# A two-block transformer on one core: the last weight tile of each chunk in other parts or in another order

## Chip, cores and metric

The kernel runs on 1 core of one Trainium2 chip. The metric is the device time of one execution in microseconds (us); lower is better.

## What is computed

The reference runs two blocks of two layers each over 256 tokens of width 1024, in float32. The first block is a gated MLP mixer, a gated feed-forward layer with a short convolution, banded attention and another feed-forward layer; the second is a mixer of attention and a recurrence, a feed-forward layer with an embedding gate, latent attention and another feed-forward layer. Nearly all of the arithmetic is products of activations with weight matrices:

```python
h = h + gmlp_mixer(rmsnorm(h, a_norm_g[l]), a_w_in[l], a_v_norm_g[l], a_w_s[l], a_b_s[l], a_w_out[l])
...
h = h + chunk_attention(rmsnorm(h, b_norm_g[j]), k_shared, v_shared, b_w_q[j], b_rel_bias[j], b_w_o[j])
h = h + conv_ffn(rmsnorm(h, f_norm_g[l]), f_w_in[l], f_conv_w[l], f_conv_b[l], f_w_down[l])
...
mix = sb_rwkv_mixer(hn, hyb_w_in[j], ...)
mix = mla_mixer(hn, positions, mla_w_down[j], ...)
h = h + conv_glu(rmsnorm_2(h, ffn_norm[i]), ffn_w_in[i], ffn_conv_w[i], ffn_conv_b[i], ffn_w_out[i])
```

## The kernel before, in words

Activations stand with their 1024 features on the partitions, in 8 tiles of 128, and the 256 tokens as columns. All weight matrices are cut into tiles of 128x128 and packed on the host, in the order of use, into 399 **chunks** of 8 tiles (128 partitions x 1024 columns, 512 KB). `w()` hands out the next tile and has the chunk two ahead (`LOOK`) prepared by `_chunk` (L406): SP issues the DMA into `raw`, ACT rounds it into `whi` (type fp32r, L418), DVE makes the remainder `wlo = raw - whi` (L419). `raw` has four buffers, `whi` and `wlo` three each. Activations are split in the same way into `xh` and `xl` (L496, L497; `hh` and `hl` in the second half of a feed-forward layer). `self.spec` is the list of the tiles handed out so far.

A product of a weight tile with an activation tile is then three products on TensorE that add up in PSUM: high weight by high activation, high weight by low activation, low weight by high activation. `gemm_tile` (L439) issues them with the weights stationary and the 256 tokens as moving columns; `self.mm` (L384) is the one line, L385, through which nearly all products of the program pass. `gemm_rows` does the same with the activations stationary and 512 weight columns moving, four tiles at a time. In the profile a product is named output <- moving, stationary operand (`g<-xh,wlo`), and each product has its own load of the stationary operand, LDWEIGHTS, listed under PEld.

PE runs in program order throughout (`pe_order`, L460); the mixers have hand-written lists of steps (`GMLP_ORDER` and others), which interleave chunks' products with the small products of the mixers. In the two layers of `ffn1`, ACT and DVE too run in program order; everywhere else a scheduler places their instructions. `gated_layer` (L800) runs the feed-forward layers: 22 pairs of output tiles with 8 weight tiles each, then the down projection over 22 tiles of `hh` and `hl`.

Of the kernel before, what the change touches and what calls it, by code (L numbers as in the profile page):

```python
# [21 lines left out]
S = 256  # L22
# [4 lines left out]
CT = 8  # L27
# [296 lines left out]
class Net:  # L324
# [114 lines left out]
    def gemm_tile(self, X, ps, name, idx, cols, first=True, k0=0, ks=None, n=None):  # L439
        n = n or len(X)  # L440
        for k in range(*(ks or (0, n))):
            xh, xl = X[k]
            wh, wl = self.w(name, idx, k0 + k * P, cols)
            self.mm(ps, wh, xh, start=first and k == 0, stop=False)
            self.mm(ps, wh, xl, start=False, stop=False)
            self.mm(ps, wl, xh, start=False, stop=k == n - 1)

    def gemm_pair(self, X, ps, name, idx, parts, late=False, mid=None, at=0):

# [1276 lines left out]
```

## Time and profile before

| | us |
|---|---|
| median of 3 runs (1316.29 to 1318.71) | 1318.56 |
| the profiled execution, its own time | 1321.39 |
| span of its instructions | 1319.6 |
| PE busy (10864 products) | 1292.5 |
| PEld busy (10864 loads of weights) | 1231.4 |
| DVE busy | 1026.5 |
| ACT busy | 781.9 |

The times in the table are of one core. PE's busy time is the union of its products' recorded durations, which overlap: a product of 256 columns is recorded with some 280 ns, while the next one starts 113 to 118 ns later. How fast PE goes is read from the starts, or from the length of a run of products divided by their number.

### The profile page before, as it was taken

How to read it: one execution, taken by the hardware profiler on the slowest of the kernel's cores; microseconds unless marked ns; L12 is line 12 of the kernel's file. 1: busy time of each engine (PE TensorE's matmuls, PEld its weight loads, DVE VectorE, ACT ScalarE, POOL GpSimd, SP SyncE). 2: the span in 40 equal slices, each digit the busy share in tenths (PEclk: the TensorE clock that was granted, in tenths of full speed). 3: DMA queues.
4: the chain of work that ended last, by engine and by line, in shares of the span. 5: the costliest groups of instructions: out<-in, count | busy, mean ns of one | idle time of the engine just before them, and what ended most of it. 6: DMA issues, size and time to landing. Idle time of an engine off the chain costs nothing.

```text
span 1319.6 us, 27125 instructions
## 1 busy us (share of the span) xinstructions
PE 1292.5 (98%) x10864; PEld 1231.4 (93%) x10864; DVE 1026.5 (78%) x2037; ACT 781.9 (59%) x1359; POOL 16.1 (1%) x48
## 2 busy tenths in 40 slices
PE   7999999999999999999999999999999999999997
PEld 5999999988899999999876799999998989999997
DVE  5889997566679998578964488897779978889656
ACT  6667665457667665448343266665557766665544
POOL 0000000000000000001100000000000000000000
PEclk9999999999999999999998799999999999999998
DMA  7566555555446556574440056565555436665551
GB/s 271 176 225 193 189 189 182 189 187 177 132 145 192 191 180 190 191 237 145 124 129 18 17 167 206 192 190 182 189 176 161 127 113 189 193 198 181 191 182 60
DMA packets 70398, 223.18 MB, mean 169 GB/s; under 512 B 13408, under 2 KB 15712, under 8 KB 70272
## 3 DMA queue, kind: packets, MB, share of 16 engines
q1 hardware_dynamic: 63312, 212.43, 50.3%
q10 hardware_dynamic: 6192, 5.34, 1.4%
q0 software_dynamic: 768, 3.67, 0.8%
q8 instruction: 85, 1.39, 0.4%
q14 instruction: 41, 0.34, 0.1%
HBM read 218.53 MB, written 2.88 MB: 168 GB/s over the span
## 4 chain that ended last, share of the span: by engine, by line
PE 92%; DVE 4%; DMA 2%; ACT 1%; issue 1%; SPq 0%; ACTq 0%; DVEq 0%
PE g L385 78%; PE s L385 6%; PE t L385 3%; PE o L385 3%; PE t L783 1%; DVE wlo L419 1%; DMA raw<-in_wall 0%; DMA b<-dZ 0%; DVE tm L1217 0%; ACT whi L418 0%; DMA dA<-b 0%; DVE sqa L171 0%; DVE xl L497 0%; DVE tm L1219 0%; DMA tm<-dA 0%
## 5 line engine op out<-in xcount | busy, mean ns | idle before, releaser
L385 PE MATMUL g<-xh,whi 128*128 128x256 f32 x2184 | 618.0, 283 | 1.4 <-ACT xh L496 1.4
L385 PE MATMUL g<-xl,whi 128*128 128x256 f32 x2184 | 610.3, 279 | 2.5 <-DVE xl L497 2.4
L419 DVE TENSOR_TENSOR wlo<-raw,whi 128x1024 fp32r<-128x1024 f32 (+1 forms) x400 | 487.8, 1221 | 160.4 <-ACT whi L418 157.4
L418 ACT ACTIVATE whi<-raw 128x1024 fp32r<-128x1024 f32 (+1 forms) x400 | 421.9, 1055 | 317.4 <-PE g L385 172.5
L385 PE MATMUL g<-xh,wlo 128*128 128x256 f32 x2184 | 609.6, 279 | 0.1
L385 PEld LDWEIGHTS g<-xh,whi 128*128 128x128 f32 x2184 | 410.7, 188 | 7.2 <-issue 4.0
L385 PEld LDWEIGHTS g<-xl,whi 128*128 128x128 f32 x2184 | 410.9, 188 | 4.0 <-DVE xl L497 3.3
L385 PEld LDWEIGHTS g<-xh,wlo 128*128 128x128 f32 x2184 | 414.1, 190 | 0.3 <-DVE wlo L419 0.3
L385 PE MATMUL g<-hh,wlo 128*128 128x256 f32 x704 | 197.8, 281 | 0.0
L385 PE MATMUL g<-hl,whi 128*128 128x256 f32 x704 | 197.8, 281 | 0.0
L385 PE MATMUL g<-hh,whi 128*128 128x256 f32 x704 | 197.8, 281 | 0.0
L385 PEld LDWEIGHTS g<-hh,wlo 128*128 128x128 f32 x704 | 135.2, 192 | 0.0
L385 PEld LDWEIGHTS g<-hh,whi 128*128 128x128 f32 x704 | 132.2, 188 | 0.0
L385 PEld LDWEIGHTS g<-hl,whi 128*128 128x128 f32 x704 | 132.2, 188 | 0.0
L277 ACT ACTIVATE hh<-pr 128x256 fp32r<-128x256 f32 x88 | 36.0, 409 | 48.7 <-DVE pr L272 48.7
L496 ACT ACTIVATE xh<-h,vec 128x256 fp32r<-128x256 f32 x80 | 39.1, 499 | 24.0 <-DVE h L560 20.9
L867 ACT ACTIVATE c<-pad,vec 128x256 f32<-128x256 f32 x88 | 47.7, 590 | 9.4 <-DVE pad L856 9.4
L874 DVE SCALAR_TENSOR_TENSOR c<-pad,vec,c 128x256 f32<-128x256 f32 x88 | 42.7, 485 | 3.1
L497 DVE SCALAR_TENSOR_TENSOR xl<-h,vec,xh 128x256 fp32r<-128x256 f32 x80 | 37.9, 481 | 6.9 <-ACT xh L496 6.8
L872 DVE SCALAR_TENSOR_TENSOR c<-pad,vec,c 128x256 f32<-128x256 f32 x88 | 42.2, 480 | 0.0
L282 DVE TENSOR_TENSOR hl<-pr,hh 128x256 fp32r<-128x256 f32 x88 | 36.9, 420 | 3.9 <-ACT hh L277 3.9
L385 PE MATMUL g<-whi,xh 128*128 128x512 f32 x68 | 29.1, 428 | 9.2 <-ACT xh L496 9.2
(375 smaller groups left out, 1396.1 us busy)
## 6 DMA issues: line engine op xcount, KB each, us to landing
raw<-in_wall SPq DMA_DIRECT2D x398, 512.0 KB, 3.5
bias<-in_bias POOLq DMA_DIRECT2D x4, 768.0 KB, 7.1
cst_c<-in_c ACTq DMA_DIRECT2D x1, 896.0 KB, 7.1
raw<-in_wall SPq DMA_DIRECT2D x2, 256.0 KB, 4.1
h<-in_x ACTq DMA_DIRECT2D x2, 256.0 KB, 4.3
h<-in_x POOLq DMA_DIRECT2D x2, 256.0 KB, 7.6
ws<-in_ws ACTq DMA_DIRECT2D x1, 512.0 KB, 8.7
bs<-in_bs ACTq DMA_DIRECT2D x1, 512.0 KB, 8.8
```

What stands on the lines that cost most here:

```text
L277: self.net.nc.scalar.activation(self.H[-1][0], self.pr, AF.Copy)
L282: self.net.nc.vector.tensor_tensor(hl, self.pr, hh.bitcast(F32), ALU.subtract)
L385: self.nc.tensor.matmul(out, lhsT=lhsT, rhs=rhs, start=start, stop=stop, skip_group_check=True)
L418: nc.scalar.activation(hi[:, s], raw[:, s], AF.Copy)
L419: self.after(nc.vector.tensor_tensor(lo[:, s], raw[:, s], hi[:, s].bitcast(F32), ALU.subtract))
L496: self.nc.scalar.activation(xh, h, AF.Copy, scale=gain)
L497: self.nc.vector.scalar_tensor_tensor(xl, h, gain, xh.bitcast(F32), ALU.mult, ALU.subtract)
L783: self.nc.tensor.transpose(pt[:, b * P:b * P + P], w[:, s * P:s * P + P], self.cst["ident"])
L867: a.activation(c0, pad[:, j, 2:], AF.Identity, bias=self.col("f_conv_b", (l,), j * KF + i), scale=cw(2, j))
L872: v.scalar_tensor_tensor(c1, pad[:, j, 1:S + 1], cw(1, j), cc[n], ALU.mult, ALU.add)
L874: v.scalar_tensor_tensor(cc[n], pad[:, j, 0:S], cw(0, j), c1, ALU.mult, ALU.add)
```

## The change

In `gemm_tile` the tile that is the last of its chunk (`o == CT - 1`) is treated by the chunk's number modulo 8 (`form`). With 0 nothing changes. With 1, 2, 3, 6 and 7 the third product, `wlo` by `xh`, is issued in two parts over the token columns: 128+128, 192+64, 64+192, 240+16 and 16+240. With 4 the order of the three is low-high, high-high, high-low, with 5 high-high, low-high, high-low. All other tiles, and `gemm_rows`, are as before.

```diff
--- before.py
+++ after.py
@@ -441,9 +441,20 @@
         for k in range(*(ks or (0, n))):
             xh, xl = X[k]
             wh, wl = self.w(name, idx, k0 + k * P, cols)
-            self.mm(ps, wh, xh, start=first and k == 0, stop=False)
+            at, o = divmod(len(self.spec) - 1, CT)
+            new, end = first and k == 0, k == n - 1
+            form = at % 8 if o == CT - 1 else 0
+            if form in (4, 5):
+                self.mm(ps, *((wl, xh) if form == 4 else (wh, xh)), start=new, stop=False)
+                self.mm(ps, *((wh, xh) if form == 4 else (wl, xh)), start=False, stop=False)
+                self.mm(ps, wh, xl, start=False, stop=end)
+                continue
+            self.mm(ps, wh, xh, start=new, stop=False)
             self.mm(ps, wh, xl, start=False, stop=False)
-            self.mm(ps, wl, xh, start=False, stop=k == n - 1)
+            cut = {1: 128, 2: 192, 3: 64, 6: 240, 7: 16}.get(form, S)
+            for c in (slice(0, cut), slice(cut, S)):
+                if c.start < S:
+                    self.mm(ps[:, c], wl, xh[:, c], start=False, stop=end)
 
     def gemm_pair(self, X, ps, name, idx, parts, late=False, mid=None, at=0):
```

By the built program 233 third products are cut (48 in 128+128, 93 in 192+64 or 64+192, 92 in 240+16 or 16+240) and the order changes in 93 chunks. Lines behind L452 stand 11 lines further down in the changed kernel.

On PE, in the first mixer, at the end of a chunk whose number is 7 modulo 8 (`g` is the sum in PSUM, `xh` and `xl` the activation's parts, `whi` and `wlo` the chunk's), the order before is this:

```order
L385 MATMUL g_738<-xl_257,whi_626 128x256
L385 MATMUL g_738<-xh_256,wlo_627 128x256
L385 MATMUL g_738<-xh_264,whi_626 128x256
L385 MATMUL g_738<-xl_265,whi_626 128x256
L385 MATMUL g_738<-xh_264,wlo_627 128x256
L385 MATMUL g_785<-xh_574,whi_683 128x256
```

and with the change:

```order
L385 MATMUL g_742<-xl_257,whi_629 128x256
L385 MATMUL g_742<-xh_256,wlo_630 128x256
L385 MATMUL g_742<-xh_264,whi_629 128x256
L385 MATMUL g_742<-xl_265,whi_629 128x256
L385 MATMUL g_742<-xh_264,wlo_630 128x16
L385 MATMUL g_742<-xh_264,wlo_630 128x240
L385 MATMUL g_790<-xh_577,whi_686 128x256
```

The chunk's last product of 256 columns has become one of 16 and one of 240 with the same weights; nothing else on PE has moved.

On PE a little earlier, at the end of a chunk whose number is 4 modulo 8, the order before is this (`t<-ws,vt` is a small product of the mixer that follows the chunk):

```order
L385 MATMUL g_584<-xl_257,whi_499 128x256
L385 MATMUL g_584<-xh_256,wlo_500 128x256
L385 MATMUL g_584<-xh_264,whi_499 128x256
L385 MATMUL g_584<-xl_265,whi_499 128x256
L385 MATMUL g_584<-xh_264,wlo_500 128x256
L385 MATMUL t_615<-ws_138,vt_143 128x128
```

and with the change:

```order
L385 MATMUL g_587<-xl_257,whi_500 128x256
L385 MATMUL g_587<-xh_256,wlo_501 128x256
L385 MATMUL g_587<-xh_264,wlo_501 128x256
L385 MATMUL g_587<-xh_264,whi_500 128x256
L385 MATMUL g_587<-xl_265,whi_500 128x256
L385 MATMUL t_618<-ws_138,vt_143 128x128
```

The product with `wlo` now stands two products earlier; their number is the same.

On ACT in the same mixer, where the scheduler places the work (`whi<-raw` prepares a chunk, `xh<-gs` the high part of a gated activation, `u<-u` the activation function), the order before is this:

```order
L418 ACTIVATE whi_586<-raw_585 128x1024
L642 ACTIVATE u_570<-u_568 128x512
L509 ACTIVATE xh_574<-gs_572 128x256
L509 ACTIVATE xh_580<-gs_578 128x256
L418 ACTIVATE whi_626<-raw_625 128x1024
L418 ACTIVATE whi_683<-raw_682 128x1024
L509 ACTIVATE xh_661<-gs_659 128x256
L642 ACTIVATE u_657<-u_655 128x512
L509 ACTIVATE xh_667<-gs_665 128x256
```

and with the change:

```order
L418 ACTIVATE whi_589<-raw_588 128x1024
L520 ACTIVATE xh_577<-gs_575 128x256
L653 ACTIVATE u_573<-u_571 128x512
L520 ACTIVATE xh_583<-gs_581 128x256
L418 ACTIVATE whi_629<-raw_628 128x1024
L520 ACTIVATE xh_664<-gs_662 128x256
L418 ACTIVATE whi_686<-raw_685 128x1024
L653 ACTIVATE u_660<-u_658 128x512
L520 ACTIVATE xh_670<-gs_668 128x256
```

The first `xh` has moved ahead of an activation function and the third ahead of the preparation of a chunk; the instructions are the same. ACT's order differs in some 35 places of this kind in the whole program and DVE's in some 60; SP's order of transfers is the same, and POOL's has one instruction moved by two places.

## Rows read from the trace of the kernel before

**Rows 1.** The page's busy times: us, share of the span, number of instructions.

```profile
PE 1292.5 (98%) x10864; PEld 1231.4 (93%) x10864; DVE 1026.5 (78%) x2037; ACT 781.9 (59%) x1359; POOL 16.1 (1%) x48
```

**Rows 2.** The page's chain that ended last, by engine and by line.

```profile
PE 92%; DVE 4%; DMA 2%; ACT 1%; issue 1%; SPq 0%; ACTq 0%; DVEq 0%
PE g L385 78%; PE s L385 6%; PE t L385 3%; PE o L385 3%; PE t L783 1%; DVE wlo L419 1%; DMA raw<-in_wall 0%; DMA b<-dZ 0%; DVE tm L1217 0%; ACT whi L418 0%; DMA dA<-b 0%; DVE sqa L171 0%; DVE xl L497 0%; DVE tm L1219 0%; DMA tm<-dA 0%
```

**Rows 3.** PE's waits: for whom, us in total, times, longest us.

```profile
PE g L385 <- ACT xh L496: 10.7, 2, 9.2
PE t L385 <- DMA b<-dZ: 2.5, 2, 2.0
PE g L385 <- DVE xl L497: 2.4, 2, 1.6
...
PE t L783 <- DVE tm L1314: 0.2, 1, 0.2
```

**Rows 4.** The same view, ACT and DVE waiting before a chunk's conversions.

```profile
ACT whi L418 <- PE g L385: 172.5, 149, 2.9
DVE wlo L419 <- ACT whi L418: 157.4, 200, 5.0
```

**Rows 5.** The chain in order of time: start us, length us, products in it.

```profile
92.14 178.41 PE g L385 x1509
...
271.23 0.69 PE t L385 x3
...
790.06 0.43 PE t L385 x2
790.49 18.05 PE g L385 x159
...
862.94 10.88 PE g L385 x96
873.82 0.34 PE s L385 x4
874.16 11.42 PE g L385 x96
885.58 0.43 PE t L385 x2
...
886.01 90.45 PE g L385 x768
...
1156.89 16.32 PE g L385 x144
...
1197.64 90.45 PE g L385 x768
```

**Rows 6.** Stretches: length, PE busy (products), granted clock, DMA share, GB/s.

```profile
95.00:270.00 175.00, 175.00 (x1484) 1.00 0.58 187
680.00:720.00 40.00, 39.23 (x499) 0.92 0.10 33
720.00:770.00 50.00, 49.13 (x328) 0.76 0.11 35
```

**Rows 7.** Groups of weight loads: busy us, mean ns | idle before, by whom.

```profile
L385 PEld LDWEIGHTS g<-xh,wlo 128*128 128x128 f32 x2184 | 414.1, 190 | 0.3 <-DVE wlo L419 0.3
L385 PEld LDWEIGHTS g<-xl,whi 128*128 128x128 f32 x2184 | 410.9, 188 | 4.0 <-DVE xl L497 3.3
L385 PEld LDWEIGHTS g<-xh,whi 128*128 128x128 f32 x2184 | 410.7, 188 | 7.2 <-issue 4.0 <-ACT xh L496 1.6 <-ACT whi L418 0.3
```

**Rows 8.** Timeline of weight loads (PEld): start us, recorded us, instruction.

```profile
48.72 0.97 PEld L385 LDWEIGHTS t<-ws,vt 128*128 128x128 f32 x8
49.61 0.19 PEld L385 LDWEIGHTS g<-xh,whi 128*128 128x128 f32 x1
...
276.21 0.19 PEld L385 LDWEIGHTS g<-whi,xh 128*128 128x128 f32 x1
276.32 0.19 PEld L385 LDWEIGHTS g<-whi,xl 128*128 128x128 f32 x1
```

## The prediction

> **What bounds the kernel now.** I read the busy times first, then the chain of work that ended last, then PE's waits, and last the timeline of PE and of its weight loads. TensorE is busy for 1292.5 us of a span of 1319.6 us [rows 1], and 92% of the chain is PE, 78% in the product groups `g` of L385 [rows 2]. PE's idle time has few causes: 10.7 us for ACT `xh`, of which one wait of 9.2 us is the start of the program, 2.5 us for a DMA, 2.4 us for DVE `xl`, and smaller ones [rows 3]. The queues that feed it are early: ACT idles 172.5 us before `whi` until PE gives a buffer back, and DVE idles 157.4 us before `wlo` [rows 4]. So what is added to PE's stream is added to the time, almost without discount, and what moves on ACT and DVE costs only where it makes PE wait.
>
> The spacing of PE's products is what matters, not their recorded duration. The pieces of the chain [rows 5] give it: 1509 products in 178.41 us are 118.2 ns each, 768 in 90.45 us are 117.8 ns, but 144 in 16.32 us are 113.3 ns, all of the same form, 256 columns against 128x128 weights, three per weight tile. **There are two cadences**, about 117.8 and 113.3 ns, and a stretch keeps the one it has until other products come between. Eight long pieces of the slow one, from the one at 92.14 to the one at 1197.64, hold 5129 products, eleven of the fast one, with the last at 1156.89, hold 1629. Over both that is (5129 x 117.8 + 1629 x 113.3) / 6758 = 116.7 ns a product. It is no matter of the granted clock, which is 1.00 in a slow stretch too [rows 6].
>
> Every product is preceded by its own load of weights; two products in a row with the same `whi` load it twice (LDWEIGHTS `g<-xh,whi` and `g<-xl,whi`, x2184 each) [rows 7]. The load for the next product runs under the present one. **How long a load takes** is seen where the products are too short to hide it: eight 128x128 loads of `ws` start at 48.72 and the next load at 49.61, 0.111 us each; the load at 276.21, behind products of one column and of the type in question, is followed by the next at 276.32, 0.11 again [rows 8]. I take 0.112 and, within the rounding of these rows, 0.109 as the lower end: nearly the whole 113 to 118 ns of a product of 256 columns. The present stream has no room for a second load under one product.
>
> **The change, part by part.** (1) *The split.* 233 third products are cut in two: 48 into 128+128, 93 into 192+64 or 64+192, 92 into 16+240 or 240+16 columns. No column is added; 233 loads and 233 products are. A part of 16 to 240 columns needs less PE time than the load that must come before the next product: the product of 512 columns takes 0.23 us (three in 0.69 us [rows 5]), so 0.45 ns a column, and even 240 columns are 0.108 us. So both parts last as long as a load, 0.112 us each, and wherever the cut lies the pair takes 0.224 us in place of 0.1167: 0.107 us more. 233 x 0.107 = **25.0 us**. The lower bound goes by the shortest load and the slow cadence, 2 x 0.109 - 0.1178 = 0.100 us, 23.3 us; the upper by the fast cadence, 2 x 0.112 - 0.1133 = 0.111 us, 25.8 us. Below these lies only the case in which the second load is hidden (a rival). I count all of it on the path: in the long pieces of rows 5, which hold most of the chunks, PE runs without a gap, and from 680 to 720 us, where hardly a weight is moved (33 GB/s [rows 6]), no cut lies by the order of the program.
>
> The Trainium skill ("TensorE: Matmul & The Clock Gate", LDWEIGHTS) puts a weight load at its columns over 1.2 GHz, 107 ns for 128; the measured 0.11 us agrees. The same page (Back-to-back issue gap) gives a product of N columns N/2.4 + 2.5 ns when it stands by itself, by which a cut would cost only the second 2.5 ns, an estimate of 0.6 us in all; that is the first rival in its words.
>
> (2) *The order.* In 93 chunks the three products of the last tile change places; same products, same loads. `wlo` is wanted up to two products (0.23 us) earlier; PE's loads wait 0.3 us in all for `wlo` today [rows 7], and `whi` and `wlo` come back to their pools at most 0.23 us later in a chunk of 24 products, 2.8 us. Cover for this is the idle time in front of both conversions [rows 4]. I take 0; if the cover were gone, 93 x 0.23 would be 21 us, but nothing in rows 4 points there.
>
> (3) *The moved work on ACT and DVE.* Where the queues are placed by the scheduler and not in program order (the mixers and the layers of ffn2), ACT and DVE get another order in some 35 and 60 places, mostly by one or two instructions, as in the fence on ACT; SP keeps its order. Each place can take away or add a wait of PE. The trace shows such waits of 0.2 to 1.6 us; the ten rows of this view without the start are 11 us in all (first and last in [rows 3]), so no more than a few us can be won. I take one such wait more, **+1.5 us**, bounds -3 and +6.
>
> (4) *The cadence.* A cut breaks the rhythm of loads, and the rhythm after a break is one of the two. If the shares stay as they are this term is 0, and I take 0. It is the largest unknown: the two bounds are the rivals below.
>
> (5) *The clock.* From 680 to 770 us the granted clock averages 0.92 and then 0.76 [rows 6], half speed in parts, about 15 us lost. Shifts of where these fall may change it by a few us either way: 0, bounds -3 and +3.
>
> Sum: 25.0 + 0 + 1.5 + 0 + 0 = 26.5 us. The profiled execution took 1321.39 us (span 1319.6 and 1.8 around it), 2.8 above the median of the three runs, 1318.56; added to the median: **1345 us**.
>
> **Rivals.** *Only columns count* (chance 0.05): the second load, of weights that are already there, is hidden or skipped. For it: the second part needs no new weights. Against it: today's pair on the same `whi` pays in full, 113 to 118 ns per product. It gives 1318.6 + 1.5 = 1320 us.
>
> *The slow cadence spreads* (0.31): after products that are shorter than a load, the trace goes on slowly: behind the four one-column products at 873.82 the 96 at 874.16 take 11.42 us, 119 ns each, where the 96 before them took 10.88 [rows 5]. If all cuts act so, the 1629 fast products of the long pieces lose 4.5 ns each, 7.3 us: 1352 us, up to 1357 with term 3 at its bound.
>
> *The fast cadence spreads* (0.10), the rival on the other side: a cut every few chunks throws the stream out of the slow rhythm. For it: behind the two products at 790.06 that are not of this kind the stream turns from slow to fast, and stays so for 159 products in 18.05 us [rows 5]; against it: the same two products at 885.58 leave it slow. 5129 x 4.5 ns = 23.1 us would come back. With the split at its lower bound and no new wait that is 1318.6 + 23.3 - 23.1 = 1319 us, not slower; it decides for "not slower" only if nearly every slow product turns fast. With half of them turned it is 1334 us.
>
> *The short parts run as plain fp32* (0.04): a product of plain fp32 with 128 columns takes two records of 0.11 us [rows 8]. If a part of fewer than 256 columns were done so, each part would be 0.22 us or more, the pair 0.33 us longer, 233 x 0.33 = 77 us: 1396 us. No product of this type with fewer than 256 columns stands in the trace, so it can't be excluded by a row.
>
> **How the numbers follow.** Forecast (shares of the cadences about as now, partly mixed) 0.50, slow spreads 0.31, fast spreads 0.10, only columns 0.05, plain fp32 0.04. The forecast's own range is 1336 to 1353. With half of the slow products turned fast at the lower end, and the slow rival with its bounds at the upper, the range for 8 in 10 is 1330 to 1358; outside are the rest of the fast rival, the columns rival and plain fp32. A measurement of this kernel tells about 0.2% (2.6 us) from no change. Slower: forecast, slow rival, plain fp32 and a part of the fast rival, 0.88. Within 0.2%: most of the columns rival and of the full fast rival, 0.08. Faster: 0.04.
>
> **What would show it.** PE has 233 products and loads more, 11097. Around a cut the loads stand 0.11 us apart and the two parts together take 0.22 us, at 128+128 as at 16+240: that shows term 1 right; 0.12 would show the columns rival. In chunks of changed order the spacing stays 113 to 118 ns. Spacings of long pieces show the cadence: the 16.32 us of 144 products growing to over 17 for the slow rival, the 178.41 us of 1509 shrinking (less their cuts) for the fast one. PE's waits in all should stay near 20 us. A total waiting of PE over 27 us would show term 3 undersized. The prediction is wrong if the pair's length depends on the cut, or if one cadence takes over.

## The result, and the profile after

The changed kernel takes 1323.27 us (median of 6 runs, 1322.58 to 1326.09) against 1318.63 us of the kernel before beside it: 1.0055 times as long, 95% interval 1.003 to 1.008. It is slower, as forecast, but by 4.6 us and not by 26.5, and 1323 lies below the range that was given. The profiled execution took 1323.33 us, with a span of 1321.5 us.

The page's busy times of the kernel after answer to [rows 1]: 233 products and 233 loads more, and PE only 1.5 us busier.

```profile
PE 1294.0 (98%) x11097; PEld 1234.9 (93%) x11097; DVE 1026.8 (78%) x2037; ACT 786.4 (60%) x1359; POOL 15.3 (1%) x48
```

PE's waits in the kernel after (for whom, us in total, times, longest us) answer to [rows 3]. All rows of this view sum to 20.9 us, before to 20.7. Single waits have changed places: the one for a DMA (2.5 us) is gone, and one for DVE `f` (2.0 us) and one for `wlo` (1.5 us) are new.

```profile
PE g L385 <- ACT xh L507: 10.8, 2, 9.2
PE s L385 <- DVE f L1193: 2.0, 1, 2.0
PE s L385 <- DVE dg L556: 1.6, 1, 1.6
PE g L385 <- DVE wlo L419: 1.5, 1, 1.5
...
PE g L385 <- DVE xl L508: 0.6, 1, 0.6
```

The chain of the kernel after in order of time (start us, length us, products) answers to [rows 5].

```profile
93.31 176.52 PE g L385 x1548
...
807.17 16.81 PE g L385 x148
...
885.17 89.52 PE g L385 x788
...
1199.35 89.52 PE g L385 x788
```

These rows hold the whole story when they are laid beside those of before. Four cuts in a piece that was fast already: 144 products in 16.32 us have become 148 in 16.81, which is 0.49 us or **0.1225 us a cut**. Twenty cuts in a piece that was slow: 768 products in 90.45 us have become 788 in 89.52. The piece is *shorter* by 0.93 us although twenty cuts were put into it. At 113.37 ns, the fast cadence, 768 products take 87.07 us (as they do in two traces below), and 87.07 + 20 x 0.1225 = 89.52. So the 748 whole and 20 cut products all run at the fast cadence now. The same for the longest piece: 1509 products would take 171.1 us fast, 39 cuts add 4.8, together 175.9; the row shows 176.52, and the 0.6 us between are in the row of before too (178.41 against 1509 x 117.8 = 177.8).

The timeline of the weight loads of the kernel after, around a cut into 192 and 64 columns and around one into 240 and 16 (start us, recorded us):

```profile
901.37 0.19 PEld L385 LDWEIGHTS g<-xl,whi 128*128 128x128 f32 x1
901.49 0.30 PEld L385 LDWEIGHTS g<-xh,wlo 128*128 128x128 f32 x2
901.71 0.19 PEld L385 LDWEIGHTS g<-xh,whi 128*128 128x128 f32 x1
901.82 0.19 PEld L385 LDWEIGHTS g<-xl,whi 128*128 128x128 f32 x1
901.94 0.19 PEld L385 LDWEIGHTS g<-xh,wlo 128*128 128x128 f32 x1
902.06 0.19 PEld L385 LDWEIGHTS g<-xh,whi 128*128 128x128 f32 x1
...
904.33 0.30 PEld L385 LDWEIGHTS g<-xh,wlo 128*128 128x128 f32 x2
904.55 0.19 PEld L385 LDWEIGHTS g<-xh,whi 128*128 128x128 f32 x1
904.66 0.19 PEld L385 LDWEIGHTS g<-xl,whi 128*128 128x128 f32 x1
904.79 0.19 PEld L385 LDWEIGHTS g<-xh,wlo 128*128 128x128 f32 x1
```

The two loads of a cut (`x2`) take 0.22 us together at either place, and the next two or three starts are 0.11 to 0.13 us apart before the stream is at 0.113 again.

Counted over the whole trace, of the steps from the start of one product of 256 columns to the start of the next, 6004 were slow (about 116 to 123 ns, 117.8 in the mean) and 2777 fast (113 to 115 ns, 113.4 in the mean) before. After, 1413 are slow and 6767 fast, and 439 of those slow ones stand within four products of a cut and so belong to its price. That leaves 974 slow steps in place of 6004: 5030 x 4.43 ns = **22.3 us come back**, against 233 x 0.1225 = **28.5 us** for the cuts.

The rest is in the stretch with the half clock. In the kernel after the granted clock is 1.00 and 0.83 where it was 0.92 and 0.76 [rows 6]:

```profile
95.00:270.00 175.00, 175.00 (x1535) 174.70 (x1535) 148.56 (x237) 108.09 (x168) 0.00 (x0) 1.00 0.62 188
680.00:720.00 40.00, 39.23 (x523) 28.22 (x522) 21.36 (x52) 18.54 (x38) 0.00 (x0) 1.00 0.13 40
720.00:770.00 50.00, 49.23 (x343) 39.24 (x344) 29.48 (x85) 17.44 (x41) 0.23 (x3) 0.83 0.17 53
```

If the products that are in both traces are matched one by one, the second trace gains 5.4 us on the first between the products at 697 and at 755 us, where half speed (1.2 GHz) was granted for 30.7 us before and for 17.1 us after. 28.5 - 22.3 - 5.4 = +0.8 us for the two profiled executions, whose spans differ by 1.9; the 1.1 us left over is not taken apart here. Whether the clock's part belongs to the change is asked below.

### The profile page after: what moved, and what is told of

Its sections match the earlier page's. It is cut to its first block, busy times and chain, and to the rows that moved or that the text cites. A ratio compares the mean times of both kernels' runs of the same rounds, so it can differ in the third digit from the quotient of the medians.

```text
span 1321.5 us, 27588 instructions
## 1 busy us (share of the span) xinstructions
PE 1294.0 (98%) x11097; PEld 1234.9 (93%) x11097; DVE 1026.8 (78%) x2037; ACT 786.4 (60%) x1359; POOL 15.3 (1%) x48
## 4 chain that ended last, share of the span: by engine, by line
PE 91%; DVE 5%; ACT 2%; issue 1%; DMA 1%; ACTq 0%; SPq 0%; DVEq 0%
PE g L385 78%; PE s L385 5%; PE t L385 4%; PE o L385 3%; DVE wlo L419 2%; PE t L794 1%; ACT whi L418 1%; DMA raw<-in_wall 0%; ACT e L736 0%; DVE xl L508 0%; DVE sqa L171 0%; DVE tm L1134 0%; DMA dA<-b 0%; DVE ple_g L993 0%; DVE f L1083 0%
## 5 line engine op out<-in xcount | busy, mean ns | idle before, releaser
L385 PE MATMUL g<-xh,wlo 128*128 128x256 f32 (+4 forms) x2354 | 607.5, 273 | 1.5 <-DVE wlo L419 1.5
L385 PE MATMUL g<-xl,whi 128*128 128x256 f32 x2184 | 603.2, 277 | 0.7 <-DVE xl L508 0.6
L385 PEld LDWEIGHTS g<-xh,wlo 128*128 128x128 f32 x2354 | 427.2, 188 | 1.7 <-DVE wlo L419 1.7
L385 PE MATMUL g<-hh,wlo 128*128 128x256 f32 (+4 forms) x760 | 195.4, 272 | 0.0
L385 PE MATMUL g<-hl,whi 128*128 128x256 f32 x704 | 193.5, 276 | 0.0
L507 ACT ACTIVATE xh<-h,vec 128x256 fp32r<-128x256 f32 x80 | 39.1, 500 | 34.5 <-DVE h L571 30.7
L878 ACT ACTIVATE c<-pad,vec 128x256 f32<-128x256 f32 x88 | 47.8, 590 | 12.5 <-DVE pad L867 12.4
L953 ACT ACTIVATE c<-pad,vec 128x256 f32<-128x256 f32 x44 | 26.5, 601 | 20.9 <-DVE pad L943 18.5
```

The source lines that it names most:

```text
L385: self.nc.tensor.matmul(out, lhsT=lhsT, rhs=rhs, start=start, stop=stop, skip_group_check=True)
L507: self.nc.scalar.activation(xh, h, AF.Copy, scale=gain)
L878: a.activation(c0, pad[:, j, 2:], AF.Identity, bias=self.col("f_conv_b", (l,), j * KF + i), scale=cw(2, j))
L953: a.activation(c0, pad[:, 1, 2:], AF.Identity, bias=self.col("ffn_conv_b_2", (l,), i), scale=cw(2))
```

## Experiments

The theory after the traces, **theory A**: a cut costs about 0.11 us (0.1225 by the rows above) and leaves PE's stream in the fast cadence, which lasts up to the next products of another kind. Rivals: **B**, a cut costs almost nothing and what follows is untouched, or it is the new order that sets the cadence; **C**, any added product does it; **D**, it takes the pair of parts; **E**, the order and the moved work on ACT and DVE cost waits of their own.

| kernel | cuts | slow steps | median us | ratio to before, 95% interval |
|---|---|---|---|---|
| before (profiled) | 0 | 6004 | 1318.63 | |
| the change | 233 | 1413 | 1323.27 | 1.0055 (1.003 to 1.008) |
| order alone | 0 | 5811 | 1317.59 | 1.0036 (1.0008 to 1.0064) |
| cuts alone | 233 | 1400 | 1322.76 | 1.0085 (1.0059 to 1.0111) |
| a cut in each 16th chunk | 23 | 2115 | 1301.31 | 0.9928 (0.9900 to 0.9957) |
| two cuts per chunk | 467 | 1495 | 1352.09 | 1.0314 (1.0259 to 1.0369) |
| 16 cuts behind breaks | 16 | 1100 | 1296.03 | 0.9834 (0.9800 to 0.9869) |
| whole product twice | 0 | 5038 | 1322.40 | 1.0024 (0.9993 to 1.0056) |
| half a product once | 0 | 4366 | 1311.45 | 0.9929 (0.9903 to 0.9954) |
| order and 16 cuts | 16 | 1069 | 1296.59 | 0.9891 (0.9855 to 0.9928) |
| 16 cuts again | 16 | 973 | 1296.68 | 0.9889 (0.9855 to 0.9923) |
| before again (one run) | 0 | 5761 | 1313.66 | |

Ratios are to runs of before on the same chip, side by side. Those had medians of 1310.7 us (22 runs), 1319.05 us (14 runs) and 1313.2 us (11 runs) in the three groups of runs, so a ratio is worth more than a median.

**The order alone.** The lines of the cut are left away:

```diff
-            cut = {1: 128, 2: 192, 3: 64, 6: 240, 7: 16}.get(form, S)
+            cut = S
```

> Only the order of the three products is changed (forms 4 and 5, 93 chunks); nothing is cut. Theory A (the cuts, and not the order, set the cadence of the stream; a cut costs 0.11 us and leaves the stream at 113.4 ns a product): within 3 us of the kernel before, and some 4500 to 7000 of the products' steps still at 117.8 ns (before: 6004). Rival B (the new order, or the reordering on ScalarE and VectorE, gives the fast cadence; the cuts cost almost nothing): fewer than 2500 steps at 117.8 ns, and about 16 to 20 us less than before.

5811 slow steps, as theory A has it: the order does not set the cadence, and rival B's form with the order falls. But the time is 0.36% above before, and the interval leaves out zero; theory A had said within 3 us. This is taken up with the last pair. The chain shows what else moved here:

```profile
91.98 178.41 PE g L385 x1509
...
808.81 16.96 PE g L385 x144
...
887.42 87.07 PE g L385 x768
```

The first long piece is slow as before. The two others have changed places with [rows 5]: 144 products that took 16.32 us take 16.96, and 768 that took 90.45 take 87.07.

**The cuts alone.** The branch for forms 4 and 5 is left away.

> Only the cuts (233, at the five places); the order stays as before in every chunk. Theory A: 1322 to 1326 us as the full change, 1000 to 2000 steps at 117.8 ns. Rival B (the order gives the cadence): some 6000 steps at 117.8 ns, and then either 1343 us (a cut costs 0.107 us) or about 1319 us (a cut costs nothing).

1322.76 us and 1400 slow steps, both as theory A has them: the full change's numbers without its order. The cuts alone give the effect. The new waits for `f` and `wlo` (2.0 and 1.5 us) are in this trace too, so they are not the order's.

**A tenth of the cuts.** Cut 128 + 128 only:

```diff
-            form = at % 8 if o == CT - 1 else 0
+            form = at % 16 if o == CT - 1 else 0
...
-            cut = {1: 128, 2: 192, 3: 64, 6: 240, 7: 16}.get(form, S)
+            cut = {1: 128}.get(form, S)
```

> One cut of 128 + 128 in the last tile of each sixteenth chunk, 25 in all, no new order. Theory A: the cuts cost 25 x 0.11 = 2.7 us; the four long stretches of before at 117.8 ns (4534 steps) turn fast from their first cut on, on average 8 chunks or 192 products in, so about 3760 steps fewer at 117.8 ns x 4.45 ns = 16.7 us: 1302 to 1308 us, faster than both kernels. Rival B (a cut has a net price of 4.6 / 233 = 0.02 us and does nothing to what follows): 1319 us, some 6000 steps at 117.8 ns.

Two of the 25 chunks turned out to be used by `gemm_rows`, so there are 23 cuts. 1301.31 us, 0.7% faster than before and just under the 1302 to 1308 of theory A. 1509 products and four cuts (1513) of the first long piece:

```profile
92.86 172.93 PE g L385 x1513
...
869.02 87.32 PE g L385 x770
```

172.93 us is 5.5 us less than the 178.41 of before; 768 products and two cuts take 87.32, and 87.07 + 2 x 0.1225 is 87.32. In this trace all 21 cuts with a clear run of products behind them are followed by the fast cadence, 6 of them after a slow one. Rival B would have left some 6000 slow steps, where 2115 are counted, and the time at that of before (1310.7 us beside it), and falls.

**Twice the cuts.** The third product is cut in the fourth and in the eighth tile:

```diff
-            form = at % 8 if o == CT - 1 else 0
+            form = at % 8 if o in (CT // 2 - 1, CT - 1) else 0
```

> Twice the cuts: the third product is cut in the fourth and in the eighth tile of the same chunks (about 466 cuts), no new order. Theory A: the fast cadence is nearly used up, so the second 233 cuts cost their full 0.11 us, 25.6 us, less at most 3 us for the last slow steps: 1345 to 1350 us. Rival B (net price of 0.02 us a cut): 1328 us.

1352.09 us, 29.3 above the cuts alone (0.125 us for each of 234 cuts) and 2 above the 1345 to 1350 of theory A, which had taken 0.11 us a cut. The spans of the two profiled executions differ by 25.5 us, 0.109 each. The piece of 768 products, now with 40 cuts, is the cleanest measure:

```profile
901.45 91.97 PE g L385 x808
```

87.07 us without a cut, 89.52 with 20, 91.97 with 40: twice the same 2.45 us, 0.1225 us a cut. The price does not fall with their number, and nothing more comes back, since the piece was fast already.

**Cuts only where the cadence may change.** The tiles were read off PE's order: the fourth tile behind each break that 72 or more products follow.

```diff
+CUT_TILES = [i + 3 for i in (64, 120, 219, 924, 1003, 1512, 1536, 1732, 1811, 2056, 2088, 2356, 2532, 2611, 2856, 2888)]
...
-            self.mm(ps, wl, xh, start=False, stop=k == n - 1)
+            cuts = (128, S) if len(self.spec) - 1 in CUT_TILES else (S,)
+            for c0, c1 in zip((0,) + cuts, cuts):
+                self.mm(ps[:, c0:c1], wl, xh[:, c0:c1], start=False, stop=k == n - 1)
```

> One cut of 128 + 128 in the fourth weight tile behind each break (sums, broadcasts, attention) that a stretch of 72 products or more follows: 16 cuts, no new order. Theory A (a cut turns the stream fast, and it stays so up to the next break): the cuts cost 16 x 0.12 = 1.9 us, some 700 to 1300 steps are left at 117.8 ns, in the short stretches, and the time is 1294 to 1300 us, at or below that of the 23 cuts in each sixteenth chunk (1301). Rival B (the fast cadence does not last, it needs a cut again and again): more than 2500 steps at 117.8 ns, 1304 us or more.

1296.03 us, and 1296.68 when it was run again (last pair): 1.1 to 1.7% faster than before, the fastest kernel of this study. Its chain:

```profile
92.92 171.87 PE g L385 x1510
...
808.49 16.32 PE g L385 x144
...
866.66 87.19 PE g L385 x769
```

One cut holds the 1500 products behind it in the fast cadence. Rival B's condition, that the cadence needs renewing, falls with the first row: 171.87 us where slow products took 178.41. Against the changed kernel this one has 217 cuts fewer, 217 x 0.1225 = 26.6 us; the spans, 1321.5 and 1292.9, differ by 28.6.

**What in the cut does it.** Two kernels put something else into the 23 places: the whole third product a second time, or only its left half. The first counts one small term twice, the second leaves out half of one.

```diff
+            at, o = divmod(len(self.spec) - 1, CT)
+            if at % 16 == 1 and o == CT - 1:
+                self.mm(ps, wl, xh, start=False, stop=False)
             self.mm(ps, wl, xh, start=False, stop=k == n - 1)
```

> In the last tile of each sixteenth chunk, 23 places, the third product is made twice at its full 256 columns (so wl x xh counts twice there), with no cut: an added product with its own load, and none that is short. Theory A (what turns the stream is a product that is shorter than the load beside it): 23 x 0.115 = 2.6 us more than before, 4000 to 6500 steps at 117.8 ns, 1310 to 1322 us. Rival C (any added product and load turns it): about 2100 steps at 117.8 ns and 1300 us, as with the cuts at the same places.

```diff
-            self.mm(ps, wl, xh, start=False, stop=k == n - 1)
+            at, o = divmod(len(self.spec) - 1, CT)
+            c = slice(0, 128 if at % 16 == 1 and o == CT - 1 else S)
+            self.mm(ps[:, c], wl, xh[:, c], start=False, stop=k == n - 1)
```

> In the last tile of each sixteenth chunk, 23 places, the third product is made over columns 0 to 127 only and the other half is left out: one short product and no added load. Theory A: one short product turns the stream, 1700 to 2500 steps at 117.8 ns, and as the product lasts as long as the load the time is that of the 23 cuts less 23 x 0.11 = 2.5 us: 1297 to 1301 us. Rival D (it takes the pair on one weight): 4000 to 6500 steps at 117.8 ns, 1308 to 1320 us.

The whole product twice leaves the cadence alone: at the 21 places with a clear run on either side, 13 were slow before it and slow behind it, 8 fast and fast. It has 5038 slow steps and 1322.40 us, just above the 1310 to 1322 expected. Two added products in a slow piece simply cost two slow steps (90.69 - 90.45 = 0.24 us), and the one long piece that is fast here (1506 products) was so from its start:

```profile
92.59 178.89 PE g L385 x1513
...
397.07 170.72 PE g L385 x1506
...
876.95 90.69 PE g L385 x770
```

Rival C falls. The half product, with 4366 slow steps and 1311.45 us, lies within both of rival D's ranges and outside theory A's, but neither side had expected how it comes to these numbers. Stretches of 39 us before, between and behind the half products at 110.5, 154.1, 199.3 and 242.8 us show why (length, PE busy and number of products):

```profile
113.00:152.00 39.00, 39.00 (x346) 39.00 (x345) 38.50 (x65) 28.30 (x46) 0.00 (x0) 1.00 0.63 201
156.00:195.00 39.00, 39.00 (x333) 39.00 (x333) 37.99 (x64) 25.78 (x43) 0.00 (x0) 1.00 0.60 190
203.00:242.00 39.00, 39.00 (x346) 39.00 (x346) 26.43 (x38) 20.33 (x29) 0.00 (x0) 1.00 0.60 194
```

346, 333, 346 products: fast, slow, fast. **One short product flips the cadence**, each time: of the 21 half products with a clear run on either side, 11 went from fast to slow and 10 from slow to fast. So theory A was wrong in saying that one short product makes the stream fast whatever it was before. Rival D was right that it takes the pair to leave it fast from either cadence, but its numbers came out because flips in both directions leave about half of the steps slow, not because the half product does nothing. Two short products do not simply flip it twice: from slow they led to fast as well (7 of 7 with the 16 cuts, 15 of 19 in the changed kernel). Why this is so is not shown by these runs.

**The kernel before in another execution.** Unchanged.

> The kernel before, unchanged, profiled in another execution. Theory A (its executions differ by the cadence that chance leaves each stretch in): another number S of steps at 117.8 ns, and a span of 1319.6 - (6004 - S) x 0.00443 us, within the 4 us that the granted clock can add or take. Rival: S near 6004 again and the same stretches slow, so that the cadence belongs to the program and not to the execution.

```profile
93.09 178.41 PE g L386 x1509
...
395.98 176.91 PE g L386 x1502
...
803.42 16.96 PE g L386 x144
...
882.03 87.07 PE g L386 x768
```

The same program (one comment line longer, hence L386), another cadence: 144 products are slow here and the 768 behind them fast, the reverse of [rows 5]. So the program does not fix the cadence of these stretches, and the rival falls for them. For others it does not: up to 359 us all 22 stretches of eight steps or more have the cadence that they had before, and the two longest pieces, half of all slow steps, are slow in both executions and with the order alone. The second of them was this before:

```profile
395.45 176.92 PE g L385 x1502
```

That piece is not slow in every program, since with the whole product twice it was fast from its start. What sets the cadence behind a break is thus partly the same from execution to execution and partly not, and these runs do not show why. The number of slow steps is 5761, though, and the span 1311.9 us, 6.6 below the 1318.5 that this number gives, beyond the 4 us allowed. Most of the rest is the clock:

```profile
680.00:720.00 40.00, 39.23 (x524) 28.30 (x522) 20.57 (x50) 17.95 (x38) 0.00 (x0) 1.00 0.09 28
720.00:770.00 50.00, 49.11 (x364) 40.08 (x364) 31.47 (x88) 18.16 (x41) 0.23 (x3) 0.86 0.20 64
```

1.00 and 0.86 in place of 0.92 and 0.76 [rows 6], with no edit at all; half speed was granted for 13.7 us here and for 30.7 us before. The clock's 5.4 us in favour of the changed kernel's trace is thus within what executions of one kernel differ by. Products matched one by one tell the same (us by which each trace is ahead, negative, or behind):

| product at (us, before) | after - before | before again - before |
|---|---|---|
| 86.2 | +1.1 | +1.0 |
| 275.9 | -0.7 | +1.0 |
| 389.5 | +1.4 | +0.5 |
| 578.3 | -0.4 | +0.5 |
| 696.9 | +1.1 | -0.5 |
| 754.6 | -4.3 | -7.1 |
| 873.7 | -0.9 | -4.0 |
| 976.3 | -1.8 | -7.4 |
| 1185.3 | +1.6 | -5.0 |
| 1287.9 | +0.8 | -8.3 |

The column of the kernel after rises where before was fast (754.6 to 873.7) and only cuts were added, and falls where before was slow (873.7 to 976.3, 86.2 to 275.9).

**The order without the chance of the cadence.** The branch for forms 4 and 5 is put into the kernel with 16 cuts, and that kernel stands beside it:

```diff
+            at, o = divmod(len(self.spec) - 1, CT)
+            form = at % 8 if o == CT - 1 else 0
+            if form in (4, 5) and len(self.spec) - 1 not in CUT_TILES:
+                self.mm(ps, *((wl, xh) if form == 4 else (wh, xh)), start=first and k == 0, stop=False)
+                self.mm(ps, *((wh, xh) if form == 4 else (wl, xh)), start=False, stop=False)
+                self.mm(ps, wh, xl, start=False, stop=k == n - 1)
+                continue
```

> The new order of the three products (92 chunks) together with the 16 cuts behind breaks, which hold the long stretches in the fast cadence, so that the order's own price is seen without the chance of the cadence. Theory A (the order costs nothing on its own; the 0.36% of the order alone came from the cadence of its executions): within 2 us of the 16 cuts alone in the same call, 700 to 1500 steps at 117.8 ns. Rival E (the order, or the moved work on ScalarE and VectorE, costs a wait here and there): 3 to 6 us above the 16 cuts alone, with PE's waits longer by as much.

> The 16 cuts behind breaks once more, as the measure for the run beside it. Theory A: 1294 to 1299 us again, its executions closer together than those of the kernel before, and 1.2 to 1.8% below the kernel before. Rival B (the first result was a lucky cadence): 1304 us or more.

1296.59 and 1296.68 us, 1069 and 973 slow steps, and PE's waits sum to 20.4 and 20.0 us. With the cadence held, the order costs nothing that these runs can tell, and rival E falls. The 16 cuts are 1.1% below before here, a little under the 1.2% that was expected. That the order alone was 0.36% above before is then most likely the chance of the cadence and the clock in the executions compared; it was measured once, and the runs don't prove it. The profiled spans of this pair, 1293.2 and 1297.5 us, differ by more than the medians, again by the granted clock: the stretch 720 to 770 has 0.96 in the first and 0.87 in the second.

## Why the prediction was wrong, step by step

- **What bounds the kernel** was right. PE's stream is the time, and the sum of PE's waits stayed (20.7 and 20.9 us). The two cadences, read off [rows 5], are the key to the result.
- **Term 1, the split**, had the right mechanism and was undersized: 0.1225 us a cut where 0.107 was taken and 0.111 was the upper bound, so 28.5 us and not 25.0. The two loads take 0.22 us as predicted. What was missing is the two or three products behind a cut, which start 0.117 to 0.13 us apart until the rhythm is back. The place of the cut matters little: from the second product before a cut to the fourth behind it, less six fast steps, the price is in the median 113 ns at 240 + 16, 120 at 16 + 240 and 123 at the three other places, or 126 there up to the sixth behind (183 cuts with a fast stretch before them).
- **The rival that only columns count** falls with the loads and with twice the cuts. The estimate of 0.6 us in all, by the gap of an isolated product in the Trainium skill ("TensorE: Matmul & The Clock Gate", Back-to-back issue gap), falls with it; the loads' 0.11 us, which agreed with that page's LDWEIGHTS section, decided. Plain fp32 falls too: no part takes 0.22 us, and 233 records have been added, where two records for each part would have added 699.
- **Term 2, the order**, was right at 0: 1296.59 against 1296.68 us with the cadence held.
- **Term 3, the moved work**, taken as +1.5 us, shows 0.2 us in the sum of PE's waits: 2.0 and 1.5 us came in as two waits, and as much went out in others.
- **Term 4, the cadence, is the step that failed.** "If the shares stay as they are this term is 0, and I take 0" was no neutral choice. The cut itself sets the cadence, nearly always the fast one, and 22.3 us came back of the 26.6 us that 6004 slow steps could give. The rival of the fast cadence had named this with its price, 23.1 us, and got 0.10, less than the slow cadence with 0.31. The evidence for those weights was how the stream goes on behind other kinds of products (two at 790.06 turned it fast, the same two at 885.58 left it slow, four of one column at 873.82 turned it slow [rows 5]). In another execution of the same program the first two of these come out the other way round, and behind the third a stream that was slow stays slow, so these rows told nothing on cuts. No row of before has a product of this type with fewer than 256 columns behind which to look. With the term so open, the range should have reached down to the full fast rival, 1319.
- **Term 5, the clock**, was 0 with bounds of 3 us, and gave 5.4 us in the profiled pair. The second execution of before gained 6.6 us in the same place, so the size was off, and it need not be of the change.
- **What would show it** worked as written: 11097 products, loads 0.11 us apart at the cut, waits near 20 us, and the long piece shrinking, 178.41 to 176.52 us with 39 cuts in it, which had been named as the sign of the fast rival. The sign of being wrong, that "one cadence takes over", came as well. That "slower" came out was luck: it is what is left of two terms of nearly the same size, of which the forecast had only one.

With the measured sizes the sum is 28.5 + 0 + 0.2 - 22.3 = +6.4 us without the clock, and +4.6 us (1.0055, up to 1.008) was measured. The 22.3 us are of one pair of executions.

## What to carry to other kernels

Where the same kind of product shows two spacings in different stretches of a trace, an edit that breaks the stream will also decide which of them follows; give that its own term and a range that reaches to both ends, and look at more than one execution before reading a stretch's spacing as a property of the program. Such an effect can be had without the edit's price: here 16 cuts, at 2 us, bring the gain for which 233 paid 28.5, and make the kernel 1.1 to 1.7% faster than before.

## What was not expected of the hardware

- Products of 256 columns with a load of weights for each have two stable spacings, 117.8 and 113.4 ns, both at a granted clock of 1.00. The stretches of 1500 products kept the one that they began with as long as no short product stood in them.
- Which one a stretch gets can differ between executions of the same program: 6004 and 5761 slow steps, with the first 359 us alike and most long stretches from 780 us on turned round. Between these two executions it makes 1.1 of the 7.7 us by which their spans differ, and the granted clock most of the rest. Beside each other on one chip the kernel before spreads by 16.7 us over 14 runs and 13.5 over 11, the one with 16 cuts by 6.7 over 4 and 5.0 over 6; that the cadence makes this difference is likely, not shown.
- One product of 128 columns in such a stream flips the spacing (21 of 21), a product cut in two on one weight leaves it fast (183 of 184 in the changed kernel where it was fast before the cut, 15 of 19 where it was slow), and an added product of 256 columns leaves it as it is (21 of 21). The cause within TensorE is open.
